# DeltaNet steps of two PSUM banks each, in fewer places between the products

## The chip, the cores and the metric

The kernel runs on one core of one Trainium2 chip. The metric is the device time of one execution in microseconds, as a median of repeated runs. TensorE is called PE here, VectorE DVE, ScalarE ACT, GpSimd POOL and SyncE SP, as in the profile.

## The reference, cut to what matters

One layer for 256 positions and a width of 2048: a gated DeltaNet branch and a short-convolution branch side by side, merged by gates, then an output projection and a SwiGLU block. The DeltaNet branch, with 16 heads of 128 columns, is what the change is about:

```python
q = l2_norm(silu(conv(q))); k = l2_norm(silu(conv(k))); v = silu(conv(v))
g = cumsum(g)                                   # log decay, per chunk
decay  = exp(where(causal, g_i - g_j, -inf))
a_low  = where(strict, (k_beta @ k.T) * decay, 0)
t_mat  = a_low + eye                            # unit lower triangular
u, w   = triangular_solve(t_mat, [v*beta, k_beta*exp(g)])
attn   = (q @ k.T) * decay
v_new  = u - w @ S;  o = q_dec @ S + attn @ v_new;  S = S*exp(g_last) + k_dec.T @ v_new
o      = rms_norm(o) * silu(z)
```

## The kernel before

**Products.** Almost all of the work is the weight products. `product` (L388) runs one: 16 row blocks of a 512-column weight slab, each as three float32r matmuls (activation high part by weight high part, low by high, high by low). The high part `wh` of a weight chunk is cast by ACT, the low part `wl` is subtracted by DVE, both in `ensure` (L299), which stays four chunks of two row blocks ahead. Products for `k` and `q` (and `v` of group 0) put channels on partitions and have 256 columns, all others 512. The order is `k0 q0 v0 k1 z0 q1 v1 k2 z1 q2 v2 k3 z2 q3 v3 scc0 z3 sch0 scb0 scc1 ...`.

**DeltaNet work.** The 16 heads go in four groups of four (`g`, `HG` = 4). For each group there are tasks, written as generators: `post_qk` (convolution, SiLU, splitting and norms of `k` and `q`; its PE work is `ssb`), `post_v` (`vt`), `decay` (the decay matrices, PE work `dec`), `core` (the rest). `core` makes the Gram matrices `gr0` and `gr1`, copies their 32x32 diagonal blocks out by ACT (`c32`), sends them through DRAM, inverts them on POOL by substitution in 62 dependent steps (`tb`, `rb`), and brings them back through DRAM as `rc`. ACT copies `rc` into `R`; `levels` then doubles the inverse twice (PE steps `z` and `y`, DVE transposes into `mt`, ACT copies into `zt` and `R`). Then come the two half-sequence solves (`u`, with `uc` between them), the outputs `o0` and `o1`, the output norm, and the transposes `oc`.

**What sets the order.** The program writes every engine's order itself. A recording layer (`Pace`) notes for every instruction an estimated cost and the estimated end on its engine. Each task holds a due time. Between chunks of a product, `step` (L346) advances each task that is due by one piece, that is, to its next `yield`. `advance` (L332) sets `pace.end` to zero, runs the piece, and takes the latest estimated end that was recorded while it ran as the task's new due time; `yield n` also asks for `n` free PSUM banks. So where a task's piece stands on PE is decided by these numbers when the program is built. `product` itself may not start while more than one earlier product still holds its PSUM banks: then `force` (L353) advances tasks in the order of their due times, due or not, until a bank pair is closed. A pair is closed by the evacuation in the product's own task (`evac_chan` for `k` and `q`, `evac_rows`, that is `rows_v` on ACT, for `v`); tickets (`turn`) make these tasks take turns. There are four small banks (`SM`) for the DeltaNet steps and two pairs for products.

A *place* is a run of DeltaNet matmuls on PE between two product matmuls.

Of the kernel before, what the change touches and what calls it, by code (L numbers as in the profile page):

```python
# [15 lines left out]
P = 128  # L16
# [4 lines left out]
HG = 4  # L21
# [32 lines left out]
class Pace:  # L54
# [7 lines left out]
    SCALAR_COST = 68.0  # L62
    DMA_ISSUE = 1200.0
# [81 lines left out]
class Lane:  # L145
# [50 lines left out]
def tile_gdn_shortconv_layer(  # L196
# [135 lines left out]
    def advance(t):  # L332
        pace.end = 0.0
# [499 lines left out]
    def decay(g):  # L833
# [8 lines left out]
        for blk in range(3):  # L842
            if blk < 2:
                gd = gp.tile([P, 2, HG, P], F32R, tag="gd", name=f"gd{blk}_{g}")
                for e in range(2):
                    for c in range(HG):
                        act.activation(
                            gd[:, e, c, :], upper, AF.Copy,
                            scale=gdec_rf[:, e, blk, HG * g + c:HG * g + c + 1],
                        )  # L850
                yield 1
            b = bank(f"dec_{g}_{blk}")
            for e in range(2):
                pe.matmul(
                    b, ones_r if blk == 1 else lower_r,
                    gd[:, e].rearrange("p c n -> p (c n)"),
                    start=(e == 0), stop=(e == 1),
                )
            bv = b.rearrange("p (c n) -> p c n", n=P)
            if blk == 1:  # L860
                for c in range(HG):
                    act.activation(
                        em[:, c, blk, :], bv[:, c, :], AF.Exp, bias=aj[:, HG * g + c:HG * g + c + 1]
                    )
            else:
                dst = em2 if blk else em[:, :, 0, :]
                act.activation(dst, bv, AF.Exp)
                pool.tensor_tensor(dst, dst, up_b, op=ALU.mult)
            yield 1
        mark(("em", g), (em, em2))  # L870

    def core(g):
# [4 lines left out]
        yield from need(("sc", g), 1)  # L877
# [5 lines left out]
        for cp in range(2):  # L883
            for c in (2 * cp, 2 * cp + 1):
                b = bank(f"gr0_{g}_{c}")
                for i, (e, f) in enumerate(THREE):
# [3 lines left out]
                    )  # L890
                dve.scalar_tensor_tensor(
# [5 lines left out]
                yield 1 + FREE  # L897
# [16 lines left out]
            yield 1 + (0 if cp else FREE)  # L914
# [51 lines left out]
        def levels(cp):  # L966
            s = slice(2 * cp, 2 * cp + 2)

            Rs = R[:, s].rearrange("p c i n -> p (c i) n")
            Ms = mt[:, s].rearrange("p c i n -> p (c i) n")  # L970

            def mirror(i, j):
                a, b = slice(SQ * i, SQ * i + SQ), slice(SQ * j, SQ * j + SQ)
                dve.transpose(out=Ms[b, :, a], in_=Rs[a, :, b])

            def each(nm, n, f, rows=P):
                bv = bank(f"{nm}_{g}_{cp}")[:rows, :4 * n].rearrange("p (x n) -> p x n", n=n)
                for x in range(4):
                    f(bv[:, x, :], x)
                return bv  # L980

            for q in range(NB):
                qs = slice(SQ * q, SQ * q + SQ)
                act.copy(Rs[qs, :, qs], rc[qs, 4 * cp:4 * cp + 4, :])
            if cp:
                mark(("R", g))
            yield 1
            for li, e in enumerate(LEVELS):
                Zs = zt[:, s].rearrange("p c i n -> p (c i) n")

                def cut(t, half):
                    return t.rearrange("p x (m h e) -> p x m h e", h=2, e=e)[:, :, :, half, :]

                def packed_row(t):
                    return t.rearrange("p (m e) -> p m e", e=e)

                for i, j in ((0, 1),) if li else ((0, 0), (1, 1), (2, 2)):
                    mirror(i, j)
                yield 1
                nm = P // (2 * e)  # L1000

                def zmm(o, x):
                    us = ud[:, 2 * cp + x // 2, x % 2, :]
                    for m in range(nm):
                        pe.matmul(
                            o[:, m * e:(m + 1) * e], us[:, (2 * m + 1) * e:(2 * m + 2) * e],
                            Ms[:, x, 2 * m * e:(2 * m + 1) * e], start=True, stop=True,
                        )

                b = each("z", P // 2, zmm, e)  # L1010
                for m in range(nm):
                    act.copy(
                        Zs[(2 * m + 1) * e:(2 * m + 2) * e, :, m * e:(m + 1) * e],
                        b[:, :, m * e:(m + 1) * e],
                    )
                yield 1
                b = each("y", P // 2, lambda o, x: pe.matmul(
                    packed_row(o), Zs[:, x, :],
                    cut(Rs, 1)[:, x], start=True, stop=True), P // 2)
                for m in range(nm):  # L1020
                    act.activation(
                        Rs[2 * m * e:(2 * m + 1) * e, :, (2 * m + 1) * e:(2 * m + 2) * e],
                        b[m * e:(m + 1) * e, :, m * e:(m + 1) * e], AF.Copy, scale=-1.0,
                    )
                if e < LEVELS[-1]:
                    yield 1
            mark(("lv", g, cp))

        for cp in range(2):
            spawn(levels(cp))  # L1030
        yield from need(("R", g), 1)
        for cp in range(2):
            yield from need(("lv", g, cp), 1)
# [12 lines left out]
        for m in range(2):  # L1046
            if m == 1:
                b = quad(f"uc_{g}", lambda o, c: pe.matmul(
                    o, ua[:, c, 0, 1, :], u[:, 0, c, :], start=True, stop=True))
                dve.tensor_tensor(v[:, 1], v[:, 1], b, op=ALU.subtract)  # L1050
                yield 1
# [3 lines left out]
            yield 1  # L1055

        yield from need(("z", g), 1)
        zs = st["z", g]
        ssq = small.tile([P, 2, HG], F32, tag="so", name=f"so_{g}")
        ov = zs  # L1060
        for m in range(2):
            def om(o, c):
                if m == 0:
                    pe.matmul(o, ua[:, c, 1, 0, :], u[:, 0, c, :], start=True, stop=True)
                else:
                    pe.matmul(o, ua[:, c, 1, 1, :], u[:, 0, c, :], start=True, stop=False)
                    pe.matmul(o, ua[:, c, 1, 2, :], u[:, 1, c, :], start=False, stop=True)
            b = quad(f"o{m}_{g}", om)
# [5 lines left out]
            dve.tensor_tensor(ov[:, m], b, zs[:, m], op=ALU.mult)  # L1074
            if m:
                mark(("done", g))
            yield 1
# [4 lines left out]
        yield 1  # L1082
        for hp in range(2):
            b = bank(f"oc_{g}_{hp}")
            bv = b.rearrange("p (h t) -> p h t", t=T)
            for j in range(2):
                for m in range(2):
                    pe.transpose(bv[:, j, m * P:(m + 1) * P], ov[:, m, 2 * hp + j, :], ident)
            sl = slice(2 * hp, 2 * hp + 2)
            split(oa[g][0][:, sl, :], oa[g][1][:, sl, :], bv)  # L1090
            if hp:
                mark(("oc", g))
            yield 1
# [333 lines left out]
```

## Time and profile before

| | |
|---|---|
| median of 3 runs | 1883.56 us (1882.84 to 1884.25) |
| the profiled execution's own time | 1883.2 us |
| its span | 1881.5 us |
| PE busy | 1867.7 us (99%) |
| DVE busy | 1275.2 us (68%) |
| ACT busy | 939.5 us (50%) |
| POOL busy | 193.4 us (10%) |
| granted PE clock, mean | 0.999 |

The profile is of one execution; its durations are those of that execution. A matmul's shown length is that of one passing through the array, and lengths overlap: the step from start to start is what PE spends on one. DeltaNet matmuls of plain float32 are shown as two passes each. Line 171 and line 190 (172 and 193 in the changed kernel) are those of the recording layer, which issues every instruction; so rows are told apart by the names of their tiles.

### The profile page before, as it was taken

Reading aid. Unit: us, or ns where it says so; the run is one execution under the profiler, and the core shown is the slowest. Engines: PE = TensorE matmul, PEld = TensorE weight load, DVE = VectorE, ACT = ScalarE, POOL = GpSimd, SP = SyncE. Lnnn points to the kernel's source line nnn. Section 1 sums busy time; section 2 is a strip of 40 time slices with the busy share of each in tenths; the row PEclk is TensorE's granted clock in tenths of the full one; section 3 lists DMA queues with packets and bytes.
Section 4 is the critical chain, followed back from the end, with each engine's and each line's share of the span. In section 5 each row is a group of like instructions: output and inputs, shape, how many; then the busy total and the mean of one; then the engine's idle time right before and its main releaser. Section 6 shows DMA issues by size and latency. Waiting matters only on the chain.

```text
span 1881.5 us, 25191 instructions
## 1 busy us (share of the span) xinstructions
PE 1867.7 (99%) x9458; PEld 1582.5 (84%) x9458; DVE 1275.2 (68%) x1808; ACT 939.5 (50%) x1244; POOL 193.4 (10%) x344
## 2 busy tenths in 40 slices
PE   9999999999999999999999999999999999999997
PEld 9999899988887888888888888888888888888886
DVE  6778688586876877445577788666666666645454
ACT  6855766667545445444444455444444444433442
POOL 0018044171250000000000000000000000000000
PEclk9999999999999999999999999999999999999999
DMA  8455355355464556665555565555555555565553
GB/s 302 158 184 190 138 171 189 121 183 173 159 204 138 200 185 213 207 205 201 188 189 190 188 204 189 208 193 192 193 197 192 191 189 191 200 217 197 191 191 133
DMA packets 100364, 354.99 MB, mean 189 GB/s; under 512 B 12177, under 2 KB 12433, under 8 KB 99985
## 3 DMA queue, kind: packets, MB, share of 16 engines
q1 hardware_dynamic: 98432, 349.69, 54.6%
q0 software_dynamic: 1664, 3.67, 0.8%
q8 instruction: 74, 1.21, 0.3%
q14 instruction: 50, 0.40, 0.1%
q10 hardware_dynamic: 144, 0.01, 0.0%
HBM read 350.18 MB, written 3.15 MB: 188 GB/s over the span
## 4 chain that ended last, share of the span: by engine, by line
PE 97%; DMA 1%; DVE 1%; ACT 1%; issue 0%; DVEq 0%; ACTq 0%
PE mm_dn L171 13%; PE mm_fg L171 13%; PE mm_fu L171 13%; PE mm_proj L171 9%; PE mm_gate L171 9%; PE mm_q L171 5%; PE mm_v L171 5%; PE mm_scb L171 5%; PE mm_out L171 5%; PE mm_z L171 5%; PE mm_sch L171 4%; PE mm_scc L171 4%; PE mm_k L171 4%; PE gr L171 1%; PE o L171 1%; PE y L171 0%
## 5 line engine op out<-in xcount | busy, mean ns | idle before, releaser
L190 DVE SCALAR_TENSOR_TENSOR wl<-raw,wh 128x1024 fp32r<-128x1024 f32 (+1 forms) x652 | 791.9, 1223 | 494.3 <-ACT wh L190 487.9
L190 ACT CAST wh<-raw 128x1024 fp32r<-128x1024 f32 (+1 forms) x652 | 679.5, 1044 | 873.3 <-PE mm_fu L171 132.5
L171 PE MATMUL mm_dn<-wh,ff 128*128 128x512 f32 x704 | 216.7, 389 | 0.0
L171 PE MATMUL mm_fg<-wh,hg 128*128 128x512 f32 x704 | 216.7, 389 | 0.0
L171 PE MATMUL mm_fu<-wh,hg 128*128 128x512 f32 x704 | 216.7, 389 | 0.0
L171 PE MATMUL mm_gate<-wh,xg 128*128 128x512 f32 x512 | 157.5, 389 | 0.0
L171 PEld LDWEIGHTS mm_dn<-wh,ff 128*128 128x128 f32 x704 | 132.1, 188 | 27.6
L171 PEld LDWEIGHTS mm_fg<-wh,hg 128*128 128x128 f32 x704 | 132.1, 188 | 27.4
L171 PEld LDWEIGHTS mm_fu<-wh,hg 128*128 128x128 f32 x704 | 132.1, 188 | 27.4
L171 PE MATMUL mm_fg<-wl,hg 128*128 128x512 f32 x352 | 136.9, 389 | 0.0
L171 PE MATMUL mm_fu<-wl,hg 128*128 128x512 f32 x352 | 136.9, 389 | 0.0
L171 PE MATMUL mm_dn<-wl,ff 128*128 128x512 f32 x352 | 136.9, 389 | 0.0
L171 PEld LDWEIGHTS mm_gate<-wh,xg 128*128 128x128 f32 x512 | 96.1, 188 | 19.9
L171 PE MATMUL mm_gate<-wl,xg 128*128 128x512 f32 x256 | 99.6, 389 | 0.0
L171 PE MATMUL mm_q<-xg,wh 128*128 128x256 f32 x512 | 93.3, 284 | 0.0
L171 PE MATMUL mm_k<-xg,wh 128*128 128x256 f32 x512 | 92.8, 284 | 0.4 <-ACT wh L190 0.4
L171 PE MATMUL mm_z<-wh,xg 128*128 128x512 f32 x256 | 81.1, 398 | 0.0
L171 PEld LDWEIGHTS mm_q<-xg,wh 128*128 128x128 f32 x512 | 80.1, 192 | 0.5
L171 PEld LDWEIGHTS mm_k<-xg,wh 128*128 128x128 f32 x512 | 79.6, 191 | 0.7 <-ACT wh L190 0.6
L171 PE MATMUL mm_sch<-wh,xg 128*128 128x512 f32 x256 | 80.1, 394 | 0.0
L171 PE MATMUL mm_scb<-wh,xg 128*128 128x512 f32 x256 | 79.7, 393 | 0.0
L171 PE MATMUL mm_scc<-wh,xg 128*128 128x512 f32 x256 | 79.5, 392 | 0.0
(256 smaller groups left out, 2983.8 us busy)
## 6 DMA issues: line engine op xcount, KB each, us to landing
raw<-in_w_in_dram SPq DMA_DIRECT2D x284, 512.0 KB, 4.2
raw<-in_w_gate_dram SPq DMA_DIRECT2D x88, 512.0 KB, 3.9
raw<-in_w_up_dram SPq DMA_DIRECT2D x88, 512.0 KB, 3.7
raw<-in_w_down_dram SPq DMA_DIRECT2D x88, 512.0 KB, 3.5
raw<-in_w_pb_dram SPq DMA_DIRECT2D x32, 512.0 KB, 4.3
raw<-in_w_pa_dram SPq DMA_DIRECT2D x32, 512.0 KB, 4.3
raw<-in_w_out_dram SPq DMA_DIRECT2D x32, 512.0 KB, 4.0
raw<-in_w_in_dram SPq DMA_DIRECT2D x8, 256.0 KB, 5.6
```

What stands on the lines that cost most here:

```text
L171: return f(*a, **k)
L190: return f(*a, **k)
```

## The change

Six pieces of the DeltaNet tasks are made larger, so that a group has 18 steps in place of 27: `decay` makes the two sums of its second block in one step; `core` makes two `gr0` in one step; `levels` is one task for both column pairs in place of two, with the `z` (and then the `y`) of both pairs in one step and two banks; `uc` and `o0` go together, the second solve with the evacuation of `o0`; both `oc` go together. The count in `yield` says how many banks the next step takes. `Pace` adds 200 ns to the estimate of an ACT instruction that also accumulates. In `advance`, the line `pace.end = 0.0` is taken out.

```diff
@@ class Pace
+    ACCUM_COST = 200.0
...
+            if key == "act" and "accum_out" in k:
+                cost += Pace.ACCUM_COST
@@ advance
     def advance(t):
-        pace.end = 0.0
         count = pace.count
@@ decay
-        for blk in range(3):
-            if blk < 2:
-                gd = gp.tile([P, 2, HG, P], F32R, tag="gd", name=f"gd{blk}_{g}")
...
+        for blk in range(2):
+            gd = gp.tile([P, 2, HG, P], F32R, tag="gd", name=f"gd{blk}_{g}")
...
+            yield 1 + blk
...
+            across = cumsum(ones_r, 1) if blk else None
+            within = cumsum(lower_r, 2 * blk)
@@ core
-        yield from need(("sc", g), 1)
+        yield from need(("sc", g), 2)
...
+                pairs.append((c, b))
+            for c, b in pairs:
                 dve.scalar_tensor_tensor(
                     out=ua[:, c, :, 0:2, :], in0=b.rearrange("p (q i n) -> p q i n", q=2, i=2),
...
-                yield 1 + FREE
+            yield 1 + FREE
@@ levels
-        def levels(cp):
...
+        def levels():
...
+                for cp, b in enumerate(each("z", P // 2, zmm, e)):
+                    for m in range(nm):
+                        act.copy(
...
+                yield 2
+                for cp, b in enumerate(each("y", P // 2, ymm, P // 2)):
...
-        for cp in range(2):
-            spawn(levels(cp))
+        spawn(levels())
@@ solves and outputs
+        solve(0)
+        yield 2
+        yield from need(("z", g), 2)
+        ov = st["z", g]
+        b = quad(f"uc_{g}", lambda o, c: pe.matmul(
+            o, ua[:, c, 0, 1, :], u[:, 0, c, :], start=True, stop=True))
+        b0 = quad(f"o0_{g}", lambda o, c: om(0, o, c))
+        dve.tensor_tensor(v[:, 1], v[:, 1], b, op=ALU.subtract)
+        yield 1
+        solve(1)
+        outs(0, b0)
+        yield 1
+        b1 = quad(f"o1_{g}", lambda o, c: om(1, o, c))
+        outs(1, b1)
...
-        yield 1
+        yield 2
+        views = []
         for hp in range(2):
             b = bank(f"oc_{g}_{hp}")
...
-            yield 1
+        mark(("oc", g))
```

No matmul is added or taken away. Over the whole program there are 91 places on PE in the kernel before and 65 in the changed one. What the order of instructions shows of them at the place where product `k3` ends and `z2` begins (a name is the tile, the group's number in it; the last number is the buffer's):

PE in the kernel before, from the end of `k3` into `z2`:

```order
L171 MATMUL mm1_k3_3522<-xg3_139,wh95_3683 128x256 x2
L171 MATMUL mm1_k3_3522<-xg3_139,wl95_3684 128x256
L171 MATMUL mm0_z2_3831<-wh96_3717,xg0_136 128x512 x2
L171 MATMUL mm0_z2_3831<-wl96_3718,xg0_136 128x512
L171 MATMUL mm1_z2_3832<-wh96_3717,xg0_136 128x512 x2
L171 MATMUL mm1_z2_3832<-wl96_3718,xg0_136 128x512
```

PE in the changed kernel, from behind the last matmul of `k3` to the first of `z2`:

```order
L172 MATMUL vt_1_0_3684<-ident_88,cv_v1_3247 128x128 x4
L172 MATMUL vt_1_1_3693<-ident_88,cv_v1_3247 128x128 x4
L172 MATMUL z_1_0_3736<-mt_145,ua_1_3121 32x32 x8
L172 MATMUL z_1_1_3745<-mt_145,ua_1_3121 32x32 x8
L172 MATMUL dec_2_0_3759<-gd0_2_3727,lower_r_122 128x512 x2
L172 MATMUL y_1_0_3768<-R_1_3237,zt_144 64x64 x4
L172 MATMUL y_1_1_3773<-R_1_3237,zt_144 64x64 x4
L172 MATMUL ssb_k2_3794<-scv_k2_3765,sel_124 32x256 x4
L172 MATMUL ssb_k2_3794<-sfc_k2_3766,sel_124 32x256 x4
L172 MATMUL dec_2_1_3807<-gd1_2_3782,ones_r_123 128x512 x2
L172 MATMUL dec_2_2_3810<-gd1_2_3782,lower_r_122 128x512 x2
L172 MATMUL mm0_z2_3827<-wh96_3581,xg0_136 128x512 x2
```

In the kernel before no DeltaNet step stands there; in the changed one `vt`, `z` and `y` of group 1 and `dec` and `ssb` of group 2 stand in one row, and the last Gram matmul of group 1 (`gr1_1_1`) stands 78 matmuls of 512 columns and the 192 of `k3` ahead of them, with no DeltaNet matmul between. The same run of names, one group on, stands between `scc0` and `z3`, with 60 matmuls of 256 columns and the 192 of `v3` and `scc0` behind `gr1_2_1`.

ACT in the kernel before, around the copies of `rc` into `R` of group 1:

```order
L190 CAST wh100_3849<-raw100_3848 128x1024
L190 ACTIVATE cv_v2_3734<-cv_v2_3734 128x512
L190 COPY R_1_3071<-rc_1_3619 32x4x32 x8
L190 CAST wh101_3876<-raw101_3875 128x1024
L190 ACTIVATE gd0_2_3892<-upper_95,gdec_rf_214 128x128 x8
L190 CAST wh102_3911<-raw102_3910 128x1024
L190 COPY zt_144<-z_1_0_3916 32x4x32 x2
L190 COPY zt_144<-z_1_1_3927 32x4x32 x2
L190 ACT_TABLE_LOAD
L190 ACTIVATE em_2_3890<-dec_2_0_3944 128x4x128
L190 ACTIVATE R_1_3071<-y_1_0_3949 32x4x32 x2
L190 ACTIVATE R_1_3071<-y_1_1_3956 32x4x32 x2
```

ACT in the changed kernel, from the same copies on:

```order
L193 COPY R_1_3237<-rc_1_3424 32x4x32 x8
L193 ACTIVATE cv_k2_3426<-cv_k2_3426 128x512 x2
L193 CAST kh_2_3252<-cv_k2_3426 128x4x256
L193 ACTIVATE gd0_2_3727<-upper_95,gdec_rf_214 128x128 x8
L193 COPY zt_144<-z_1_0_3736 32x4x32 x2
L193 COPY zt_144<-z_1_1_3745 32x4x32 x2
L193 ACT_TABLE_LOAD
L193 ACTIVATE em_2_3725<-dec_2_0_3759 128x4x128
L193 ACTIVATE cv_k2_3426<-cv_k2_3426 128x1024
L193 CAST scv_k2_3765<-cv_k2_3426 128x1024
```

and on from there:

```order
L193 ACTIVATE R_1_3237<-y_1_0_3768 32x4x32 x2
L193 ACTIVATE R_1_3237<-y_1_1_3773 32x4x32 x2
L193 ACTIVATE gd1_2_3782<-upper_95,gdec_rf_214 128x128 x8
L193 ACTIVATE em_2_3725<-dec_2_1_3807,aj_215 128x128 x4
L193 ACTIVATE em2_2_3726<-dec_2_2_3810 128x512
L193 ACTIVATE cv_q2_3819<-full_q2_3431,wc_126 128x256 x4
L193 ACTIVATE rows_v2_3824<-mm0_v2_3132,rx_135 128x512
```

Between the same steps the kernel before has casts of weight chunks (`wh`), one or two at a time; in the changed one none stands from `R` to `rows_v2`, which empties the bank that `z2` writes, and the convolution of `k2`, the splitting of it and the start of `q2` stand among them.

## Rows read from the trace of the kernel before

**Rows 1.** the page's first part: busy us (share of the span) and instructions
```profile
PE 1867.7 (99%) x9458; PEld 1582.5 (84%) x9458; DVE 1275.2 (68%) x1808; ACT 939.5 (50%) x1244; POOL 193.4 (10%) x344
```

**Rows 2.** who PE waited for: us in total, times, longest us
```profile
PE oc L171 <- DVE zs L190: 1.3, 4, 0.7
```

**Rows 3.** chain that ended last, in order of time: start, length, what
```profile
292.31 23.03 PE mm_k L171 x192
...
508.64 21.76 PE mm_scc L171 x96
```

**Rows 4.** PE in order of time, two y steps, one o step: start, length
```profile
208.44 0.40 PE L171 MATMUL mm_z<-wl,xg 128*128 128x512 f32 x1
208.77 0.68 PE L171 MATMUL y<-R,zt 128*64 128x64 f32 x8
...
209.95 0.40 PE L171 MATMUL mm_z<-wl,xg 128*128 128x512 f32 x1
...
218.20 1.15 PE L171 MATMUL y<-R,zt 128*64 128x64 f32 x16
...
231.47 0.39 PE L171 MATMUL mm_z<-wl,xg 128*128 128x512 f32 x1
231.69 1.95 PE L171 MATMUL o<-u,ua 128*128 128x128 f32 x16
...
233.94 0.39 PE L171 MATMUL mm_z<-wl,xg 128*128 128x512 f32 x1
```

**Rows 5.** PE in order of time: the last Gram matmul of group 1
```profile
249.63 0.28 PE L171 MATMUL gr<-kl,kh 128*128 128x256 f32 x1
```

**Rows 6.** POOL in order of time: substitution of group 1, two steps in it
```profile
266.13 0.23 POOL L190 TENSOR_TENSOR tb<-rb,ub 128x31 f32<-128x31 f32 x1 [4.32 <-DMA ub<-d]
...
290.42 1.17 POOL L190 TENSOR_TENSOR tb<-rb,ub 128x65 f32<-128x65 f32 x1
...
292.08 0.30 POOL L190 TENSOR_TENSOR tb<-rb,ub 128x60 f32<-128x60 f32 x1
...
302.66 2.35 POOL L161 DMA_DIRECT2D d<-rb  x4 [0.29 <-POOL rb L190]
308.97 0.93 POOL L161 DMA_DIRECT2D rc<-d  x1 [3.95 <-DMA d<-rb]
```

**Rows 7.** DMA issues: what, queue, count, size, median us to landing
```profile
rc<-d POOLq DMA_DIRECT2D x4, 128.0 KB, 3.5
```

**Rows 8.** ACT in order of time, 201 to 320 us: start, length
```profile
201.40 2.45 ACT L190 ACTIVATE gd<-upper,gdec_rf 128x128 fp32r<-128x128 f32 x8
...
204.81 0.52 ACT L190 COPY zt<-z 32x128 f32<-32x128 f32 x2
205.34 1.28 ACT L190 ACT_TABLE_LOAD   x1
206.64 0.60 ACT L190 ACTIVATE em<-dec 128x512 f32<-128x512 f32 x1
...
261.52 1.05 ACT L190 CAST kh<-cv_k 128x1024 fp32r<-128x1024 f32 x1
...
272.14 1.71 ACT L190 ACTIVATE cv_q<-full_q,wc 128x256 f32<-128x256 f32 x4
...
292.14 1.26 ACT L190 ACTIVATE rows_v<-mm_v,rx 128x512 f32<-128x512 f32 x2
...
319.38 2.52 ACT L190 COPY R<-rc 32x128 f32<-32x128 f32 x8
```

**Rows 9.** DVE in order of time, beside the POOL step at 290.42
```profile
290.06 1.36 DVE L190 SCALAR_TENSOR_TENSOR wl<-raw,wh 128x1024 fp32r<-128x1024 f32 x1
```

**Rows 10.** stretches after the last matmul: busy of each engine, PEclk, DMA
```profile
1874.00:1875.00 1.00, 0.00 (x0) 0.00 (x0) 0.86 (x5) 0.00 (x0) 0.00 (x0) 1.00 0.02 8
...
1876.00:1877.00 1.00, 0.00 (x0) 0.00 (x0) 0.62 (x1) 0.00 (x0) 0.00 (x0) 0.50 0.58 215
```

**Rows 11.** PE in order of time: the first matmuls of the run
```profile
1.44 4.31 PE L461 MATMUL warm<-ident 128*128 128x128 f32 x20 [1.44 <-POOL ident masks.py:199]
```

More of the change, by code (lines that the diff above doesn't have):

```diff
@@ new lines, in decay, with cumsum @@
+            yield 1 + blk
+            def cumsum(left, nm):
+                b = bank(f"dec_{g}_{nm}")
+                for e in range(2):
+                    pe.matmul(
+                        b, left, gd[:, e].rearrange("p c n -> p (c n)"),
+                        start=(e == 0), stop=(e == 1),
+                    )
+                return b.rearrange("p (c n) -> p c n", n=P)
+            across = cumsum(ones_r, 1) if blk else None
+            within = cumsum(lower_r, 2 * blk)
+            if blk:
+                for c in range(HG):
+                    act.activation(
+                        em[:, c, 1, :], across[:, c, :], AF.Exp,
+                        bias=aj[:, HG * g + c:HG * g + c + 1],
+                    )
@@ L869, in decay @@
+            dst = em2 if blk else em[:, :, 0, :]
+            act.activation(dst, within, AF.Exp)
+            pool.tensor_tensor(dst, dst, up_b, op=ALU.mult)
             yield 1
@@ L883, in core @@
         for cp in range(2):
+            pairs = []
             for c in (2 * cp, 2 * cp + 1):
@@ L913, in core @@
                 )
-            yield 1 + (0 if cp else FREE)
+            yield 1 if cp else 2 + FREE
         mark(("gram", g))
@@ new lines, in levels, with zmm @@
+        def levels():
+            Rs, Ms, Zs = (
+                [t[:, 2 * cp:2 * cp + 2].rearrange("p c i n -> p (c i) n") for cp in range(2)]
+                for t in (R, mt, zt)
+            )
+            def each(nm, n, f, rows=P):
+                views = []
+                for cp in range(2):
+                    b = bank(f"{nm}_{g}_{cp}")[:rows, :4 * n].rearrange("p (x n) -> p x n", n=n)
+                    for x in range(4):
+                        f(b[:, x, :], cp, x)
+                    views.append(b)
+                return views
+            for cp in range(2):
+                for q in range(NB):
+                    qs = slice(SQ * q, SQ * q + SQ)
+                    act.copy(Rs[cp][qs, :, qs], rc[qs, 4 * cp:4 * cp + 4, :])
+            mark(("R", g))
+            for li, e in enumerate(LEVELS):
+                nm = P // (2 * e)
+                yield 1
+                for cp in range(2):
+                    for i, j in ((0, 1),) if li else ((0, 0), (1, 1), (2, 2)):
+                        a, b = slice(SQ * i, SQ * i + SQ), slice(SQ * j, SQ * j + SQ)
+                        dve.transpose(out=Ms[cp][b, :, a], in_=Rs[cp][a, :, b])
+                yield 2
+                def zmm(o, cp, x):
@@ L1006, in zmm @@
                             o[:, m * e:(m + 1) * e], us[:, (2 * m + 1) * e:(2 * m + 2) * e],
-                            Ms[:, x, 2 * m * e:(2 * m + 1) * e], start=True, stop=True,
+                            Ms[cp][:, x, 2 * m * e:(2 * m + 1) * e], start=True, stop=True,
                         )
[L1010 to L1014, printed above, removed]
-                    )
@@ L1016, in levels @@
[L1016 to L1026, printed above, removed]
@@ L1031, in core @@
+                yield 2
+                for cp, b in enumerate(each("y", P // 2, ymm, P // 2)):
+                    for m in range(nm):
+                        act.activation(
+                            Rs[cp][2 * m * e:(2 * m + 1) * e, :, (2 * m + 1) * e:(2 * m + 2) * e],
+                            b[m * e:(m + 1) * e, :, m * e:(m + 1) * e], AF.Copy, scale=-1.0,
+                        )
+            mark(("lv", g))
+        spawn(levels())
         yield from need(("R", g), 1)
-        for cp in range(2):
-            yield from need(("lv", g, cp), 1)
+        yield from need(("lv", g), 1)
@@ L1044, in quad, with solve @@
             return bv
[L1046 to L1051, printed above, removed]
+        ssq = small.tile([P, 2, HG], F32, tag="so", name=f"so_{g}")
+        def solve(m):
             b = quad(f"u_{g}_{m}", lambda o, c: pe.matmul(
@@ L1054, in core, with om, outs @@
             act.copy(u[:, m], b)
[L1055 to L1068, printed above, removed]
+        def om(m, o, c):
+            if m == 0:
+                pe.matmul(o, ua[:, c, 1, 0, :], u[:, 0, c, :], start=True, stop=True)
+            else:
+                pe.matmul(o, ua[:, c, 1, 1, :], u[:, 0, c, :], start=True, stop=False)
+                pe.matmul(o, ua[:, c, 1, 2, :], u[:, 1, c, :], start=False, stop=True)
+        def outs(m, b):
             for c in range(HG):
```

69 lines of the change are left out of this document (17 added, 52 removed).

## The prediction

> **What bounds the kernel now.** I read the page's first part, then who waits for whom on PE, then the chain in order of time, then PE's own order around single steps. PE is busy for 99% of the span [rows 1], and the only DeltaNet wait of more than half a microsecond in all is the `oc` transposes' for DVE, 1.3 us over four groups [rows 2]. So the time is the sum of PE's starts: whole products of 96 matmuls of 512 columns at 21.76 us, or 192 of 256 columns at 23.03 us [rows 3], and between them the DeltaNet steps. A change can take time away only where a step costs PE more than its own passes; it can add time wherever PE is made to wait, since nearly all of PE's waits are hidden today.
>
> **What a place costs.** From the low-part matmul ahead of a step to the low-part matmul behind it three product starts lie, 0.68 us at 21.76/96. Around `o` it is 233.94 - 231.47 = 2.47 us, so the step cost 1.79 us for 16 passes, 0.112 us each; its own length, 1.95 us for fifteen starts and one matmul of 0.275, gives the same 0.112 [rows 4]. A place of `u`, `uc`, `o` or `gr` kind thus has no fixed price, and joining two gives nothing. Around `y` it is 209.95 - 208.44 - 0.68 = 0.83 us for 8 passes, and 8 further passes add 1.15 - 0.68 = 0.47 us [rows 4], so a `y` or `z` place (64 or 32 columns of the array) has a fixed price of 0.36 us. By the order, 22 places hold a `z` or `y` now and 16 such switches are left, since several column pairs stood together already. **Joining: -2.2 us.** With both `oc` banks behind one wait, up to 1.3 us can go; I take -0.5.
>
> **What the order does beside that.** The line that set `pace.end` to zero before each advance is gone. A task's next due time is now the latest end of anything recorded so far, and POOL's substitution of 62 dependent steps puts that far ahead. So from the last Gram place of group 1 to the end of product `k3` no DeltaNet place stands on PE, and then eleven rows of forced work follow at once, because `product` cannot start `z2` until the queue of open banks is shorter (`force`). The same piece returns at the end of `scc0` for group 2. PE has nothing else queued there: it waits for every link. That is two long stalls, in three terms.
>
> *POOL's part.* In the kernel before, the last Gram matmul starts at 249.63 [rows 5], the substitution runs from 266.13 to 302.66 and the DMA that brings `rc` back is issued at 308.97 [rows 6], landing 3.5 us later [rows 7]: 62.8 us from Gram to `rc`, today under products. In the new order PE has 78 matmuls of 512 columns (17.7 us) and the product `k3` (23.0) in that time, 40.7 us, and about 0.9 us of waiting at the start of `k3`: 41.6. For group 2 it has 60 of 256 columns (7.2) and two products (43.5): 50.7. Could the substitution be faster? A step with no long DVE instruction beside it took 0.30 us, one beside a 1.36 us low-part subtraction 1.17 [rows 6, 9]. All 62 unhindered, with some 0.08 us between them, would be 24 us in place of 36.5; the difference is 14 hindered steps. In `k3` DVE issues one such subtraction in each 2.9 us and little else, so about 12 remain: I take 61 us from Gram to `rc`, with 50 and 66 as ends (none hindered; four more hindered). PE then waits 61 - 41.6 = **19.4 us** and 61 - 50.7 = **10.3 us**. The Trainium skill bears on this (SBUF — State Buffer, section "Who interferes with whom"): a DVE instruction with two SBUF inputs and a GpSimd instruction that reads SBUF block each other for a whole instruction. By that rule the steps run free once DVE has run out of work in the stall, and the sum would come out by up to some 8 us under mine in each stall; the two row prices agree with the rule, and no row shows the chain beside an idle DVE.
>
> *ACT's part.* When `rc` is there, ACT's queue as the order gives it runs down to the evacuation that frees the bank of `z2`, and PE's links (`z`, `dec`, `y`, `ssb`) mostly finish while ACT is at the next item. By [rows 8]: `R` 2.52, two halves of SiLU at the 0.60 of the 512-column `em`, 1.2, `kh` 1.05, `gd` 2.45, `zt` two pairs 1.04, table load 1.28, `em` 0.60, the square and `scv` at the price of `kh`, 2.1, `R<-y` at the price of `zt`, 1.04, `gd` 2.45, then about 0.55 until PE's `dec` is through, four `em` pieces at the 0.3 of a `gd` piece, 1.2, `em2` 0.60, `cv_q` 1.71 and half of `rows_v`, 0.63. The sum is **20.4 us**, once per stall. Covered today by products; here nothing covers it, since ACT took the items strictly in this order, with `R` in front.
>
> *PE's own work in the stall* is not lost: 8 transposes, 32 passes of `z`, 6 of `dec`, 16 of `y`, 8 of `ssb` are some 5.3 us that PE also spends in the kernel before. Net: 19.4 + 20.4 - 5.3 = **34.5 us**, and 10.3 + 20.4 - 5.3 = **25.4 us**.
>
> **Smaller waits.** At six product starts (`z1`, `q2`, `k3`, `q3`, `sch0`, `scb1`) and at a few low parts behind a forced DVE chain, the evacuation is now issued just ahead of the product. At `z1`, for instance, `gd` 2.45, `cv_q` 1.71 and 0.63 stand on ACT against some 3 us of PE work, a wait of 1.7. Laid out alike, the others come to 0.8 to 2.6 us each; nine places in all, about **+12 us**, with 6 and 18 as ends.
>
> **Clock.** After the last matmul the granted clock stood at 1.00 until 1875 us and at 0.50 from 1876, some four idle microseconds later [rows 10]; both stalls are longer. At the start of the run 20 transposes took 4.31 us [rows 11], 0.215 each at half speed, and the products behind them ran at full. So each stall ends with up to 4.3 us at 1.2 GHz, 2.2 us lost, and 0.3 in its last `dec`: **+5 us**, ends 0 and 10.
>
> **Sum.** 34.5 + 25.4 + 12 + 5 - 2.2 - 0.5 = +74. The profiled execution took 1883.2 us (span 1881.5), 0.4 below the median of the three timed runs, which I neglect: 1883.2 + 74 = about **1957 us**.
>
> **Rivals.** *No POOL wait.* If the substitution ran unhindered throughout (50 us, or less with quicker DMAs), the waits are 8 and 0, and the joint sum is 74 - 21 = +53, with smaller waits at their lower end +47: 1930 to 1936. For it: the two prices in [rows 6]; against it: eight subtractions in `k3` still meet it. The time is below forecast, but still far above before. *Longer tail.* While ACT and DVE work off the forced piece, no weight groups are split beyond the four that are ready (11 us of PE work at 2.72 us each); if they are late again behind it and the clock stays at half over that stretch, each stall costs 10 us more: 1977. Against it: ACT needs only 1.05 us for a group. *Faster after all.* The other side: `rc` is back before PE comes to the forced piece. This decides at 41.6 us from Gram to `rc`; below it, and with ACT's items done one by one under `v2` and `k3`, nothing is left but the joining. If then every removed place gave the 0.36 us of the `y` rows, 26 places (91 now, 65 then) give 9.4 us and `oc` 1.3: 1872.5; if only `z` and `y` do, 1880.5, within 0.2%. Against it: 62.8 us measured, and an order in which ACT's items stand behind `R`, not ahead of it.
>
> **How the numbers follow.** Forecast case 0.80; no POOL wait 0.10; longer tail 0.05; no stall 0.05, of which 0.03 faster and 0.02 the same. A difference of 0.2% (3.8 us) is about what a measurement of this kernel can tell from no change. So faster 0.03, same 0.02, slower 0.95. The low end takes POOL's lower end (-20.8 us) and a little from the small waits, 1934; the high end POOL's higher end (+10), small waits at 18 and the clock at its end, 1978.
>
> **What would show it.** In the changed kernel's profile: PE idle before the first `z` of group 1 of 15 to 25 us, released by DVE's `mt` or ACT's `R`, which hang on `rc`; another of 5 to 15 us for group 2; a run of waits of 0.5 to 4 us behind each, down to the first matmul of `z2` and `z3`, released by ACT's `rows_v`; granted clock 0.50 in both stretches; from `scc2` on the same length as before; `u` and `o` passes at 0.112 us. I am wrong if PE is still busy for 99%, if the gap ahead of `z` is under 5 us (POOL's term), or if the piece behind `rc` is much shorter than 20 us (ACT's term).

## The result, and the profile after

The changed kernel takes 1946.2 us (median; 1944.1 to 1947.9), the kernel before 1883.5 us on the same chip. The ratio is 1.033, with a 95% interval of 1.0322 to 1.0345. The forecast was 1957 us in a range of 1934 to 1978, and slower. The profiled execution took 1946.9 us with a span of 1945.1, that is 63.7 us more than the profiled one of before.

The page of the changed kernel: the first part, PE and its clock in 40 slices, and the engines' shares of the chain that ended last.

```profile
PE 1883.1 (97%) x9458; PEld 1592.1 (82%) x9458; DVE 1274.5 (66%) x1808; ACT 936.7 (48%) x1243; POOL 173.7 (9%) x344
...
PE   9999996896999999999999999999999999999998
...
PEclk9999998897999999999999999999999999999999
...
PE 86%; POOL 4%; ACT 4%; issue 3%; DMA 2%; DVE 1%; SPq 0%; DVEq 0%; POOLq 0%; ACTq 0%
```

The same shares of the chain in the kernel before:

```profile
PE 97%; DMA 1%; DVE 1%; ACT 1%; issue 0%; DVEq 0%; ACTq 0%
```

PE has the same 9458 instructions as in [rows 1], but a share of 97% in place of 99%. What is lost lies in slices 7 to 10 (290 to 490 us), where the clock has fallen too. On the chain that ended last POOL, which had no share before, has 4%, and ACT 4% in place of 1%. Who PE waited for (us in total, times, the longest) says it by name:

```profile
PE z L172 <- DVE mt L193: 21.6, 6, 12.9
PE mm_z L172 <- ACT rows_v L193: 7.3, 3, 3.0
PE dec L172 <- ACT gd L193: 6.4, 6, 2.4
PE ssb_k L172 <- ACT scv_k L193: 4.6, 2, 2.3
PE mm_q L172 <- ACT zs L193: 2.6, 2, 1.5
PE mm_q L172 <- DVE wl L193: 2.1, 1, 2.1
```

In the kernel before, the only DeltaNet wait over half a microsecond was the 1.3 us of `oc` [rows 2]. PE in order of time at the two stalls (start, length, what, and in brackets the idle time before it and what ended it):

```profile
318.70 1.03 PE L172 MATMUL vt<-ident,cv_v 128*128 128x128 f32 x8
332.64 0.29 PE L172 MATMUL z<-mt,ua 128*32 128x32 f32 x2 [12.90 <-DVE mt L193]
...
352.23 1.22 PE L172 MATMUL mm_z<-wh,xg 128*128 128x512 f32 x2 [3.02 <-ACT rows_v L193]
...
468.12 0.29 PE L172 MATMUL z<-mt,ua 128*32 128x32 f32 x2 [7.68 <-DVE mt L193]
...
487.70 1.22 PE L172 MATMUL mm_z<-wh,xg 128*128 128x512 f32 x2 [3.02 <-ACT rows_v L193]
```

From the end of `k3` to `z2` it is 33.5 us, and the same piece for group 2 (459.4 to 487.7) is 28.3 us. ACT over the first of them, and where it begins the second:

```profile
331.86 2.52 ACT L193 COPY R<-rc 32x128 f32<-32x128 f32 x8 [9.96 <-DMA rc<-d]
...
348.39 1.14 ACT L193 ACTIVATE em<-dec,aj 128x128 f32<-128x128 f32 x4 [0.89 <-PE dec L172]
...
467.34 2.52 ACT L193 COPY R<-rc 32x128 f32<-32x128 f32 x8 [4.85 <-DMA rc<-d]
```

So each stall has two parts that lie end to end: up to 331.86 (467.34) ACT waits for `rc`, that is, for POOL's substitution and its two transfers; from there to the first matmul of `z2` (`z3`) ACT works without a break but one. The second part is 352.23 - 331.86 = 20.4 us, and 487.70 - 467.34 = 20.4.

### The profile page after: what moved, and what is told of

The parts are those of the page before. It is cut to its first block, busy times and chain, and to the rows that moved or that the text cites. A ratio compares the mean times of both kernels' runs of the same rounds, so it can differ in the third digit from the quotient of the medians.

```text
span 1945.1 us, 25164 instructions
## 1 busy us (share of the span) xinstructions
PE 1883.1 (97%) x9458; PEld 1592.1 (82%) x9458; DVE 1274.5 (66%) x1808; ACT 936.7 (48%) x1243; POOL 173.7 (9%) x344
## 3 DMA queue, kind: packets, MB, share of 16 engines
q8 instruction: 74, 1.21, 0.2%
## 4 chain that ended last, share of the span: by engine, by line
PE 86%; POOL 4%; ACT 4%; issue 3%; DMA 2%; DVE 1%; SPq 0%; DVEq 0%; POOLq 0%; ACTq 0%
PE mm_dn L172 12%; PE mm_fg L172 12%; PE mm_fu L172 12%; PE mm_proj L172 9%; PE mm_gate L172 9%; PE mm_z L172 5%; PE mm_scb L172 5%; PE mm_out L172 4%; PE mm_sch L172 4%; PE mm_q L172 3%; PE mm_k L172 3%; PE mm_scc L172 3%; PE mm_v L172 2%; POOL rb L193 2%; POOL tb L193 2%
```

## The experiments

**The missing line alone.** One line is put back into the changed kernel; all joined steps stay.

```diff
     def advance(t):
+        pace.end = 0.0
         count = pace.count
```

> The changed kernel with one line put back: the carried end is set to zero at the start of each advance, as in the kernel before. All joined steps stay; a group still has 18 steps. Theory (the missing line alone makes the two stalls, because a due time then holds the end of POOL's substitution): no DeltaNet work is left to be forced at the ends of k3 and scc0, both stalls and the small waits at product starts go. Of 91 places 72 remain and of 22 z or y switches 16: 6 x 0.36 us less, and the waits at oc about as long as before, so 1883.5 - 2.2, give or take 1.5: 1880 to 1884 us. Rival A (the two-bank steps are the cause: a step that needs two free banks comes late and bunches up): the stalls stay in some form and the time is above 1920 us. Rival B (every removed place is worth the 0.36 us of a z or y switch): 19 places fewer, 1883.5 - 6.8 = 1876.7 us.

Measured: 1886.65 us, ratio to the kernel before 1.0019 (1.0010 to 1.0028). Both stalls are gone, so they come from the line and not from the two-bank steps. But the joined steps don't even win the 2.2 us; the time is 2.7 us above the upper end that the theory gave. Who PE waited for names two places:

```profile
PE oc L172 <- DVE zs L193: 3.3, 6, 1.7
PE mm_sch L172 <- ACT scc L193: 1.5, 1, 1.5
```

The `oc` waits are 2 us longer than in [rows 2], and the one at the start of `sch` is new. The first is taken up again below, where a third loss is found beside it.

**The line alone, the other way round.** The kernel before, nothing joined, without the line.

```diff
     def advance(t):
-        pace.end = 0.0
         count = pace.count
```

> The kernel before with that one line taken out and nothing joined. Theory (the line alone is the cause): the same forced run of z, dec, y and ssb stands behind k3 and behind scc0, with POOL's substitution in front of it; the wait before the first z of group 1 is 11 to 15 us, the whole about as long as the changed kernel, 1940 to 1955 us. Rival A (the two-bank steps are the cause): within a few microseconds of 1883.5 us.

Measured: 1950.7 us, ratio 1.0359 (1.0345 to 1.0373). PE at the end of `k3`:

```profile
337.83 0.29 PE L171 MATMUL z<-mt,ua 128*32 128x32 f32 x2 [19.26 <-DVE mt L190]
...
349.28 1.22 PE L171 MATMUL mm_z<-wh,xg 128*128 128x512 f32 x2 [4.32 <-ACT rows_v L190]
```

The time is that of the changed kernel and a little more; the first wait was longer than I had put it (19.3 against 11 to 15), the piece behind it shorter. The wait is longer because the last Gram matmul of group 1 starts only 34.2 us ahead of the end of `k3` there (283.36; 42 in the changed kernel), and from it to `R` it is 53.7 us. With the run before, the line is shown to be the cause from both sides.

**Which of the carried ends.** The changed kernel without the reset, but what POOL will have done is not carried from task to task.

```diff
         self.end = max(self.end, end)
+        if eng != "pool":
+            self.carry = max(self.carry, end)
...
     def advance(t):
+        pace.end = pace.carry
         count = pace.count
```

> The changed kernel, in which the carried end still is not set to zero, but POOL's estimated ends (the substitution and the transfers that POOL issues) are left out of what is carried from one task to the next; ends on PE, ACT and DVE are carried as in the changed kernel. Theory (of all carried ends only POOL's 62-step substitution lies far enough ahead to do harm): no stall; 67 places, 16 z or y switches; laid along the order with the measured durations, waits are some 2 us shorter than in the kernel before, and 6 x 0.36 us of switches go: 1883.5 - 4 = 1879.5 us, 1877 to 1883. Rival (carrying any end makes tasks late, POOL's being only one): a good part of the 63 us stays, above 1900 us.

Measured: 1884.0 us, ratio 1.0003 (0.9994 to 1.0012). No stall is left: of all the ends that are carried, POOL's do the harm. That it is the 62 dependent steps among them, which last 36.5 us in the kernel before [rows 6], is argued from their length; the run leaves out all of POOL's ends. The size was missed again, by 4.5 us, and again `oc` waits. POOL, DVE and PE in order of time, around the `oc` of group 0:

```profile
241.32 2.55 POOL L196 TENSOR_TENSOR zs<-zs,ng 128x512 f32<-128x512 f32 x2 [19.80 <-ACT zs L196]
...
241.43 1.21 DVE L196 TENSOR_TENSOR rsu_o<-rsy_o 128x8 f32<-128x8 f32 x1
...
242.67 1.22 DVE L196 TENSOR_TENSOR rsu_o<-rsu_o,rsh_o 128x8 f32<-128x8 f32 x1
...
243.93 0.17 DVE L196 SCALAR_TENSOR_TENSOR rsy_o<-rsu_o,rsy_o 128x8 f32<-128x8 f32 x1
...
245.77 0.30 PE L175 MATMUL oc<-ident,zs 128*128 128x128 f32 x1 [1.73 <-DVE zs L196]
```

Two DVE steps of eight columns take as long as the POOL multiplication that runs beside them, 1.2 us in place of 0.17. DVE's chain for the output norm is late by 2.1 us, and `oc`, at the end of it, waits 1.7.

**POOL's multiplication out of the way.** The kernel of that run, in which the multiplication of `zs` by the norm weight is left out for group 1 and still counted by the planner (`planned` records a cost and issues nothing).

```diff
-            pool.tensor_tensor(
+            (planned["pool"] if g == 1 else pool).tensor_tensor(
                 zs[:, m], zs[:, m], ng.unsqueeze(1).broadcast_to([P, HG, P]), op=ALU.mult
             )
```

> The kernel of the run that leaves POOL's ends out, without POOL's two multiplications of zs by the norm weight for group 1 (128x512, 1.3 us each; the output of that group then lacks the weight). The planner counts them, so the order on every engine stays. In that run they start at 241.32, and two 8-column DVE steps of the output norm of group 0 beside them take 1.21 and 1.22 us in place of 0.17; the oc transposes behind that chain then wait 1.73 us. Theory (POOL holds DVE up there): the two take 0.17, the chain is 2.08 us shorter, the wait is under 0.3 us, and the time 1.7 us less than that run, 1884.0 - 1.7 = 1882.3 us. Rival (DVE's chain is late for another reason): the oc wait stays above 1.2 us.

Measured: 1880.75 us beside 1883.1 for the kernel before, ratio 0.9987 (0.9979 to 0.9996): 3.1 us better against the kernel before than with the multiplication.

```profile
242.04 0.17 DVE L196 TENSOR_TENSOR rsu_o<-rsu_o,rsh_o 128x8 f32<-128x8 f32 x1
...
244.28 1.63 PE L175 MATMUL oc<-ident,zs 128*128 128x128 f32 x8
```

The two steps take 0.17 and `oc` doesn't wait at all. The piece from the product matmul behind one Gram place to the next Gram place (four product steps, `oc`, four more) takes 247.19 - 242.85 = 4.3 us here and 250.25 - 242.44 = 7.8 with the multiplication. Of these 3.5 us 1.9 lie ahead of `oc`. The other 1.6 lie behind its start: 0.2 in a second wait between the transposes, the rest where the granted clock had fallen to half. The stretch with the multiplication, then without it (busy time of PE, PEld, DVE, ACT, POOL, then the granted clock):

```profile
247.00:249.50 2.50, 2.50 (x12) 2.50 (x13) 2.50 (x5) 1.13 (x2) 0.00 (x0) 0.50 0.00 0
```

```profile
247.00:249.50 2.50, 2.50 (x18) 2.02 (x17) 2.50 (x5) 1.27 (x2) 0.00 (x0) 1.00 0.51 180
```

So what the joined kernel had missed is this collision: the wait that it makes, and some 1.4 us more by the half clock behind it. The 3.5 us are 3.1 in the whole time because this run comes to the place 0.4 us later. The kernel with the line put back has the same wait (1.71 us) and the same fall (0.50 from 249 to 252 us), up to 1.7 us by half of the stretch. With 2.0 at `oc`, 1.5 at `sch` and -2.2 for the joins that is 3.0 of the 3.4 us by which it is slower than the kernel before.

**POOL's part by subtraction.** The changed kernel with half of the substitution left out, which the planner still counts, so that every other engine has the same order.

```diff
         for j in range(SQ - 1):
...
-            pool.tensor_tensor(
+            lane = planned["pool"] if j % 2 else pool
+            lane.tensor_tensor(
```

> The changed kernel in which every second step pair of POOL's substitution is left out (31 instructions of 62; the inverse is then wrong). The planner still counts their cost, so the order on every engine stays. Theory (POOL's chain is what the first part of both stalls waits for): the chain takes some 16 us in place of 31.8 and 34.3, rc lands before ACT comes to it, and the 9.96 and 4.85 us that ACT's R waits for rc go: 1946.2 - 14.8 = 1931.4 us, 1928 to 1934, a bit less if the clock falls for a shorter time. The ACT part behind R stays 20.4 us in each stall. Rival (something else would be late in rc's place): less than 7 us are gained, above 1939 us.

Measured: 1931.55 us, 14.65 less than the changed kernel. ACT and PE at the end of `k3`:

```profile
318.98 2.17 ACT L193 ACTIVATE v<-vt,vs 128x128 f32<-128x128 f32 x8
320.99 2.50 ACT L193 COPY R<-rc 32x128 f32<-32x128 f32 x8
```

```profile
322.54 0.28 PE L172 MATMUL z<-mt,ua 128*32 128x32 f32 x2 [3.56 <-DVE mt L193]
...
341.33 1.22 PE L172 MATMUL mm_z<-wh,xg 128*128 128x512 f32 x2 [3.02 <-ACT rows_v L193]
```

`R` follows `v` with no wait for `rc`. The gain is ACT's own idle time ahead of `R` (9.96 and 4.85 us), not PE's whole gap, since ACT has 2.2 us of `v` to do first. From `R` to `z2` it is still 341.33 - 320.99 = 20.3 us: the two parts are independent and lie end to end.

**ACT's part.** The changed kernel with `gd` as one ACT instruction in place of eight, counted by the planner as before.

```diff
-                    act.activation(
+                    planned["act"].activation(
                         gd[:, e, c, :], upper, AF.Copy,
...
+            nc.scalar.activation(
+                gd.rearrange("p e c n -> p (e c) n"), upper.unsqueeze(1).broadcast_to([P, 2 * HG, P]),
+                AF.Copy, scale=0.0001,
+            )
             yield 1 + blk
```

> The changed kernel in which the eight ACT pieces of each gd (2.45 us) are one instruction of 1024 columns with a constant scale (1.05 us, the price of kh, the same size); the decay is then wrong. The planner counts the old cost, so the order on every engine stays. Theory (behind rc each stall is the sum of ACT's items one after the other): gd stands twice in each, so 2 x 2 x 1.40 = 5.6 us less, and up to 1.4 us at the start of z1, behind gd: 1946.2 - 7.0 = 1939 us, 1938 to 1941. From the first R to the first matmul of z2 (of z3) 17.6 us in place of 20.4. Rival (PE's own links or DVE end the piece, ACT is beside them): less than 2 us are gained, above 1944 us.

Measured: 1941.2 us, 5.0 less. ACT in order of time:

```profile
330.98 2.52 ACT L193 COPY R<-rc 32x128 f32<-32x128 f32 x8 [10.90 <-DMA rc<-d]
...
345.14 1.14 ACT L193 ACTIVATE em<-dec,aj 128x128 f32<-128x128 f32 x4 [1.31 <-PE dec L172]
```

With the first matmul of `z2` at 348.98, the piece behind `rc` is 18.0 us, 2.4 shorter than 20.4 and not 2.8: ACT's second `gd` comes so early that its wait for PE's `dec` grows from 0.89 to 1.31. So the piece is ACT's sum, but with one link through PE; 0.8 us of the 2.0 missed lie there, over both stalls. Ahead of the stall the wait at the start of `z1` is gone, and the last Gram matmul of group 1 starts 1.8 us earlier (274.81 against 276.63); but `R` starts only 0.9 earlier, since POOL's way took 56.2 us here in place of 55.2, and ACT's wait for `rc` grew from 9.96 to 10.90. The same happens in group 2 (8.77 us of PE waiting ahead of `z` in place of 7.68). These two lose 2.0 us; 0.4 more than expected was won ahead of the stall, and 0.9 behind it, where from `z2` to `q3` it is 34.15 us in place of 35.04. With the 0.8 that makes 1.5 us; the profiled executions missed 1.7 (5.3 won of 7.0), the medians 2.0. Why POOL's way is longer here no run took apart.

**The clock.** The changed kernel with further matmuls of 128x512 in the waits, into the banks of the steps that wait, where they are overwritten.

```diff
+                    if nm == "z" and e == LEVELS[0] and not cp:
+                        fill(b, {1: 53, 2: 31}.get(g, 0))
...
+                if g > 1:
+                    fill(b, (11, 0, 5)[nm])
...
+        if nm in ("k2", "k3"):
+            fill(sb, 12)
```

> The changed kernel with further matmuls of 128x512 where PE waits in the two stalls: 53 (31) ahead of the first z of group 1 (2), 11 ahead of dec, 12 ahead of ssb, 5 ahead of the last dec, all into the step's own bank and overwritten. At 0.227 us each they fill most of the waits (12.9 and 7.7 us ahead of z, 2.4 and 2.3 behind) and no link has to come later. Theory (the fall of the clock costs the matmuls behind the stall): the granted clock stays at 1.00 through most of both stalls, so the 5.6 and 3.2 us at half speed behind the first matmul of z2 and z3 go (2.8 and 1.6 us saved), and the passes of dec that ACT waits for are shorter (about 0.5 each): 1946.2 - 5.4 = 1940.8 us, 1939 to 1944. Rival (the clock is not what these matmuls lack, or falls all the same in the last wait of 3 us): 1945 us or more.

Measured: 1947.5 us, 1.3 more than without; with 1945.6 to 1948.7 beside 1944.1 to 1947.9 that is no difference clear of the spread. PE at `z2`, and stretches of its clock (busy time of PE, PEld, DVE, ACT, POOL, then the granted clock):

```profile
332.95 0.22 PE L172 MATMUL z<-mt,ua 128*32 128x32 f32 x2 [1.34 <-DVE mt L193]
...
352.87 0.95 PE L172 MATMUL mm_z<-wh,xg 128*128 128x512 f32 x2 [2.85 <-ACT rows_v L193]
```

```profile
330.00:350.00 20.00, 15.22 (x97) 10.19 (x96) 5.71 (x14) 16.37 (x43) 1.40 (x2) 1.00 0.02 7
...
354.00:356.00 2.00, 2.00 (x9) 1.21 (x8) 2.00 (x4) 0.00 (x0) 0.00 (x0) 0.50 0.03 8
```

The clock now stays at full through the first stall (in the second it fell near the end), and `z2` still starts 352.87 - 332.95 = 19.9 us behind `z` (19.6 without). ACT where it waits for `dec`, in the first and in the second stall:

```profile
348.43 1.14 ACT L193 ACTIVATE em<-dec,aj 128x128 f32<-128x128 f32 x4 [0.59 <-PE dec L172]
...
486.60 0.60 ACT L193 ACTIVATE em<-dec 128x512 f32<-128x512 f32 x1 [1.76 <-PE dec L172]
```

The first wait is 0.89 us without the filling: inside the stall the slow PE costs 0.3 us at this one link, and nothing else, since ACT sets the pace. The second wait is new, and one of 0.48 us stands at the same item in the first stall: the five matmuls ahead of the last `dec` make it late, against what I had expected. These 2.2 us are more than the whole difference. Behind the stall the clock falls after all, behind the wait of 2.85 us that could not be filled. The rival held: what the fall costs is mainly the stretch behind the stall, and this filling did not buy it back. What a clock kept up would win without the late `dec` the run does not show.

**What a change of steps costs.** In the kernel before, eight matmuls are put ahead of each bank of `z`, `y`, `u`, `uc` and `o`: four large ones like a product's and four small ones like the step's own, all overwritten. First in two groups, then alternating at `z` and `y`, then alternating at `u`, `uc` and `o`.

```diff
+    def extra(b, small, apart):
...
+        for f in (large, small) * 4 if apart else (large,) * 4 + (small,) * 4:
+            f()
```

> The kernel before with eight further matmuls ahead of each bank of z, y, u, uc and o (52 banks in all, 16 of z, 16 of y, 20 of the others): four of 128x512 float32r like those of the products (0.227 us each by 21.76/96), then four small ones of the step's own shape. They write the step's bank and are overwritten. It is the base for the next two, which have the same instructions in another sequence. 52 x 4 x 0.227 = 47 us for the large ones and, at 0.03 to 0.06 a matmul for z and y and 0.112 for u, uc and o, some 15 us for the small ones: 1883.5 + 62 = 1945 us, 1935 to 1955.

> As the run with the extra matmuls in groups, but at the 32 banks of z and y the four large and the four small ones alternate: three further changes from a product's kind of matmul to a z or y and back at each bank, 96 in all; no matmul is added. Theory (a change to z or y and back has a fixed price of 0.36 us): 96 x 0.36 = 34.6 us more than with groups. Rival (no fixed price; the y rows of the kernel before showed something else): less than 5 us more.

> As the run with the extra matmuls in groups, but at the 20 banks of u, uc and o the four large and the four small ones alternate: 60 further changes and back. Theory (these plain 128-column steps have no fixed price, so that joining them gives nothing): within 3 us of the run with groups. Rival (they cost what z and y cost): 60 x 0.36 = 21.6 us more.

Measured: 1964.9 us in groups, 1997.3 with `z` and `y` alternating, 1964.7 with `u`, `uc` and `o` alternating. So 96 changes to a `z` or `y` and back cost 32.4 us, 0.34 each; 60 changes to a plain 128-column step cost -0.3 us, that is nothing. The base itself came 20 us above the estimate: I had counted a small plain float32 matmul as one pass, and it is two, which is some 17 us of it. PE at one `z` bank when they alternate, in order of time:

```profile
222.27 0.33 PE L1021 MATMUL z<-mt,ua 128*64 128x64 f32 x2
222.53 0.50 PE L256 MATMUL z<-xg,lower_r 128*128 128x512 f32 x1
222.96 0.33 PE L1021 MATMUL z<-mt,ua 128*64 128x64 f32 x2
```

One large and two small passes are 222.96 - 222.27 = 0.69 us; 0.23 for the large one and 0.12 for the two passes ([rows 4]: 0.47 for eight) leave 0.34 for the change there and back.

**The one join that pays.** The kernel before, with `levels` of the changed kernel and nothing else.

```diff
-        for cp in range(2):
-            spawn(levels(cp))
+        spawn(levels())
         yield from need(("R", g), 1)
-        for cp in range(2):
-            yield from need(("lv", g, cp), 1)
+        yield from need(("lv", g), 1)
```

> The kernel before, with its reset line, in which only levels is taken from the changed kernel: z of both column pairs in one step, and y likewise. 86 places, 16 z or y switches in place of 22; dec, gr, uc, o and oc stand as before. Theory (this is the one join that pays): 6 x 0.36 = 2.2 us less, 1883.3 - 2.2 = 1881.1 us, 1879 to 1883. Rival (a two-bank z or y step brings waits of its own): 1884 us or more.

> The kernel before with only levels joined, once more beside the kernel before, for a narrower interval. Theory: six z or y switches fewer, 2.0 to 2.9 us faster. Rival: the difference of the first comparison was chance, within 1 us.

Measured: 1880.5 us in both, beside 1883.2 and 1883.1: ratios 0.9985 (0.9976 to 0.9994) and 0.9987 (0.9978 to 0.9997). It is 2.6 us faster than the kernel before and 66 us faster than the changed one, about what six `z` and `y` changes at 0.34 to 0.36 us are worth. It is the best whole version of this study, by a margin near the end of what can be measured.

## Why the prediction was right

The direction, the cause and both places were as predicted; the time was 11 us lower than forecast. Step by step:

- **POOL's part: right mechanism, over by 8.6 us.** PE's path to the stall was 42 us (41.6 forecast) and 51.3 (50.7). But from the last Gram matmul to `R` it was 331.86 - 276.63 = 55.2 us and 59.3, not 61. The waits are 13.2 and 7.9 us in place of 19.4 and 10.3. For group 1 the 5.8 us come in three pieces. The way into the substitution took 15.6 us (16.5 before, [rows 5, 6]). The way out, from the issue of its result at 324.36 to `R`, took 7.5 us in place of 9.8, because both transfers landed sooner (2.9 us from the issue of `rc` to `R` against 3.5, [rows 7]). The chain itself took 32.1 us where my 61 left it 34.7. That last one was a miscount: one low-part subtraction in each 2.9 us of `k3` over the 26.4 us from the chain's start to the end of `k3` is 9, and I took 12. The trace has nine subtractions and nine long POOL steps. DVE and POOL, the last of them and the chain behind it:

```profile
316.98 1.23 DVE L193 SCALAR_TENSOR_TENSOR wl<-raw,wh 128x1024 fp32r<-128x1024 f32 x1 [1.66 <-ACT wh L193]
318.12 4.98 DVE L193 SCALAR_TENSOR_TENSOR cv_k<-full_k,wc,cv_k 128x255 f32<-128x255 f32 x12
```

```profile
317.13 1.21 POOL L193 TENSOR_TENSOR tb<-rb,ub 128x48 f32<-128x48 f32 x1
...
319.27 0.36 POOL L193 TENSOR_TENSOR rb<-rb,tb 128x49 f32<-128x49 f32 x1
...
328.98 0.92 POOL L162 DMA_DIRECT2D rc<-d  x1 [2.27 <-DMA d<-rb]
```

  Behind it no step is longer than 0.36 us. The Trainium skill (SBUF — State Buffer, section "Who interferes with whom") has DVE with two SBUF inputs and a reading GpSimd block each other for a whole instruction; the nine pairs agree. The twelve DVE steps of 255 columns behind them do not: they have two SBUF inputs too, but follow each other by 0.42 us, as where POOL is idle (2.45 us for six at 205.47), and no POOL step begun beside them takes more than 0.36. So the trace shows the hold for the long subtraction, and not for every such instruction. I had weighed the rule as up to 8 us less per stall and then left it out of the sum; 2.6 us of the chain were its part.
- **ACT's part: right.** 20.4 us forecast, 20.4 measured in both stalls, item by item from the prices of [rows 8]. That it agrees so closely is in part luck: the wait for `dec` was 0.89 us where I had put 0.55 here, and the other items came to 0.4 less than their prices. The run with the short `gd` shows that the piece follows ACT's sum, with one link through PE.
- **PE's own work in the stall: 5.3 us taken.** Net, the two stalls come to 13.2 + 20.4 - 5.3 = 28.3 and 7.9 + 20.4 - 5.3 = 23.0 us, 51.3 together, where 59.9 was forecast.
- **Smaller waits: right in sum.** At `z1`, `q2` (start and a low part), `k3`, `q3`, `sch0`, `scb1` and `oc` PE waited 11.2 us (1.3 of the `mm_z` row, 2.6, 2.1, and 1.0, 1.6, 1.5, 1.1 in rows not shown), against 1.3 in the kernel before: 9.9 more, 12 forecast. With the line back only those at `sch` and `oc` are left.
- **Clock: right in size, one place missed.** It was granted 0.50 in both stalls and for a stretch behind each:

```profile
324.00:331.00 7.00, 0.00 (x0) 0.00 (x0) 0.00 (x0) 0.00 (x0) 3.33 (x6) 0.50 0.13 31
...
352.23:357.80 5.57, 5.57 (x24) 4.32 (x25) 4.88 (x11) 1.25 (x3) 0.00 (x0) 0.50 0.25 94
...
487.70:490.91 3.21, 3.21 (x9) 2.17 (x10) 3.21 (x7) 0.52 (x1) 0.00 (x0) 0.50 0.00 0
```

  Half of 5.57 and of 3.21 us is 4.4 us lost behind the stalls, where I had 2.2 for each; a third fall that I had not seen coming, inside `q2`, adds up to 1.7 (last section). The 0.3 us in each last `dec` were lost too, but lie in ACT's 20.4 already: its wait is 0.89 us, and 0.59 with the clock kept up. I had taken the 2.2 from the 20 transposes at the start [rows 11] as run at half speed. Their 0.215 us is twice the 0.11 of one `vt` transpose (eight in 1.03), but the profile gives a granted clock of 1.00 for that stretch, so that half speed rests on their length alone.
- **Joining: `z` and `y` right, `oc` wrong.** The fixed price of 0.36 us from [rows 4] is 0.34 by the alternating runs, and none for the plain steps; the kernel with only `levels` joined won 2.6 us. For `oc` I had taken -0.5; it is -0.2 in the changed kernel (1.1 us against 1.3), and in the two joined kernels without stalls it turned to +0.6 and +2.0 us (1.9 and 3.3), mostly through a collision of POOL and DVE that a moved place brings about, which I had no term for, nor for the 1.4 us of half clock behind it.
- **The sum.** 51.3 + 9.9 + 4.4 + 1.7 - 2.2 = 65.1, and the profiled executions differ by 63.7. The 1.4 us between them are not settled; the 5.3 us of PE's own work is the term least well measured.

Of the rivals, "no POOL wait" is nearest to what came: its direction (quicker substitution) was real, for 5.8 and 1.8 us of its 20. The longer tail did not appear: 3 to 6 us at half clock, no late weights. What the runs leave open is why the wait of 1.5 us at the start of `sch` comes with the joined steps; no run took it apart.

## What to carry to other kernels

Joining small steps between large products is worth only what a switch really costs: price it first, by alternating the same instructions (0.34 us for a narrow step here, nothing for a full-width one). In a program whose order is written by a planner, one line of its bookkeeping can weigh thirty times as much as the steps that the change is about; look in the new order for runs of dependent work with nothing queued behind, and sum the slowest engine's items along them. Filling a wait can keep the clock up, but wins little while another engine sets the pace, and loses time where the filling stands ahead of a link. A short wait can cost more than its length, when the clock falls behind it (1.9 us and some 1.4 more at `oc`).

## What the runs showed of the hardware that I had not expected

- Tiny DVE instructions can be held as long as a large POOL instruction beside them: eight columns took 1.21 to 1.27 us in place of 0.17, each beside a 128x512 multiplication on POOL of about 1.3 us. It hit forms with one SBUF operand named by the trace as well, in the changed kernel with the line put back:

```profile
242.89 2.53 POOL L193 TENSOR_TENSOR zs<-zs,ng 128x512 f32<-128x512 f32 x2 [19.69 <-ACT zs L193]
...
242.94 1.27 DVE L193 TENSOR_SCALAR rsu_o<-rst_o 128x8 int32<-128x8 int32 x1
...
244.24 1.21 DVE L193 TENSOR_SCALAR rsy_o<-rsu_o 128x8 int32<-128x8 int32 x1
```

  The same section of the Trainium skill lists `tensor_scalar` among the forms that can contend with GpSimd; these rows agree.
- The clock fell after short waits too. In the changed kernel PE waited 2.10 us inside `q2` (until 257.48), and a little later the granted clock stood at half with PE busy throughout; in the run with filled waits it fell behind a wait of 2.85 us, and in the joined kernel without POOL's carried ends behind one of 1.73 us, where it stood at half for some 3.3 us (246.6 to 249.9) and cost some 1.4. The stretch in the changed kernel:

```profile
259.00:262.00 3.00, 3.00 (x16) 3.00 (x15) 2.62 (x15) 1.18 (x2) 0.00 (x0) 0.50 0.75 284
```
